# A hybrid attention block: last neighbourhood keys and queries before the last two gates, softmax sums from a ones column in v, gates by row, 368 keys

## The chip, the cores and the metric

The kernel runs on one core of a Trainium2 chip. Six agents matter: TensorE (matmuls, PE in the profile; its weight loads are PEld), VectorE (DVE), ScalarE (ACT), GpSimd (POOL), SyncE (SP), which issues nearly all DMAs here, and the DMA engines. Matmul results land in PSUM, eight banks of 128 partitions by 512 fp32; everything else lives in SBUF. The metric is the device time of one execution in microseconds, as the median of three runs.

## The reference

The kernel computes one encoder layer for 1024 tokens of width 1024, in fp32 accuracy:

```python
h = x @ W_in                       # q_a k_a v_a z_a (512 each), q_b (512) k_b v_b (128 each) z_b (512)
y_a = neighborhood_attention(q_a, k_a, v_a, rel_bias)   # 8 heads of 64, grid of 16 rows x 64 columns, window 8 x 16
y_b = windowed_gqa_with_sink(rotary(q_b), rotary(k_b), v_b, sink)   # 8 query heads, 2 kv heads, |i - j| <= 128
mixed = concat(y_a * silu(z_a), y_b * silu(z_b))
x = layer_norm(2 ** 0.25 * x + mixed @ W_out)
```

In the neighbourhood attention a query at (row, column) sees 8 rows by 16 columns, clamped inside the grid. With tokens put in column-major order (16 rows per column), a block of 128 queries is 8 grid columns, and the keys that any of them can see are 23 columns for an inner block (368 keys), 16 columns for the first and the last block (256 keys).

## The kernel before

**Number format.** Every fp32 operand is split into two fp16 tiles, high part and rest (`hi` and `lo` in the code), and a product takes three matmuls: high x high, high x rest, rest x high. ACT usually makes the high part, DVE or POOL the rest.

**Projections.** `W_in` is cut into 21 slices of 128 output columns, named after what they make: `q0..q3`, `k0..k3`, `z0..z3` for the neighbourhood heads (two heads a slice), `qb0..qb3`, `kb`, `zb0..zb3` for the banded heads. `ORDER` lists them. `project(name)` is a generator of 48 matmuls: two halves of 512 tokens, each 8 k-tiles x 3 matmuls into one of two `pj` PSUM banks. When a half is complete, `evac` queues its evacuation: for k and q `split_k` and `split_q` (L250 on ACT and L256 on DVE, each for two heads, so four operations a half; for k POOL also copies both parts to the other 64 partitions, L298); for z a tanh on ACT (L344) and a product on DVE (L345), the half of a SiLU. A new half waits until the half before the last has left its bank. The first six slices and v are made before the attention starts; the other fifteen fill it.

**Attention.** There are 128 units: 64 of the banded group b, then 64 of the neighbourhood group a, each a head (pair p, head j of it) and a block t of 128 queries. A unit goes through steps on every engine:

- `stage_qk`: two score matmuls (L797, L798) into one of four `s` banks, against 256 or 384 keys; then one DVE operation (L805) adds the bias or mask, takes the row minimum `nm` and writes `sn`.
- `stage_exp`: ACT's exponential (L821) writes back into the bank; its accumulator output (a separate read instruction) gives the row sum into a column of `sm`.
- `stage_tr`, a unit later: ACT and DVE split the probabilities into fp16 high part and rest (L829, L830), and SP issues a transposing DMA (L833).
- `stage_pv`, for four units at once: value matmuls (L856) of the transposed blocks (as weights, with a load each) against v, 64 columns each, 33 for a quad of four units.
- `stage_on`: DVE takes the reciprocal of the four row sums (L862) and multiplies (L865).
- `stage_ot`, after both heads: four PE transposes (L876) and one DVE operation that multiplies the result into the gate tile z (L879 for group b, L882 for group a, where z holds tokens by row and the attention result is by column, so z is addressed with a stride of 64 elements).

v is made first, split into `vt` tiles by ACT and DVE (L695, L686), stored to the DRAM buffer `vd`, and gathered per head pair in column order (`gather_v`, tile `va`). The bias of a head (`bias`, 896 columns for the three kinds of block, `BWIN`) is loaded per head and scaled on POOL (L773).

**What sets the order.** The program order on every engine is written out by hand in the main loop over steps i, one unit a step. `FILL_AT` gives for each filling slice the step at which its 48 matmuls begin, so that slice n is spread over the steps `FILL_AT[n]` to `FILL_AT[n + 1]`; `pump_to` places them between the score matmuls. The four engine queues `queues` hold evacuations and other small work, and a few of these are popped in each step. `m_queue`, `wo_split` and `WO_LD` place the splits of the gated tiles and of `W_out`. From step 121 on the filling work is the first output matmuls (`out_head`, L1002); the rest of them, the residual and the layer norm stand in `final()`, where the last gate, the split of the last gated tile (L910) and eight splits of `W_out` (L961, L967) run on DVE beside output matmuls on PE.

```python
ORDER = ["zb0", "z0", "zb1", "kb", "qb0", "z1", "qb1", "zb2", "qb2", "k0", "qb3", "zb3", "q0", "k1", "q1",
         "k2", "q2", "z2", "k3", "q3", "z3"]
FILL = ORDER[NPRO:]                 # NPRO = 6
FILL_AT = [0, 8, 17, 25, 33, 41, 49, 57, 66, 74, 81, 89, 97, 105, 112, 121, 123.5, 126, 128, 131, 136]
```

Pair p of the neighbourhood group has the units 64 + 16 p to 79 + 16 p.

## Time and profile before

| | |
|---|---|
| median of three runs | 449.97 us (449.89 to 451.79) |
| the profiled execution | 448.97 us |
| its span, first to last instruction | 447.2 us, granted clock 0.997 |
| busy time in the span | PE 437.1, DVE 349.0, ACT 309.9, POOL 212.0 us |
| share of the 16 DMA engines on SP's main queue | 65.8% |
| attention, first to last score matmul | 121.3 to 358.0 us |

Times are counted from the start of the span. Busy time of PE is modelled: a matmul's row lasts from its start to its drained end, and the next one starts earlier, so the distance of starts tells the true rate. A row of a group gives line, engine, operation, tiles and shapes, the number of instructions, then their busy time in us and the mean duration of one in ns, then the engine's idle time just before them and what ended it. A row of waits gives the total, the number of times and the longest. In a timeline the columns are start, duration, engine, line, operation, and in brackets the idle time before with its releaser.

### The profile page before, as it was taken

What the parts mean: (1) busy time and instruction counts of PE and PEld (TensorE: products, weight loads), DVE (VectorE), ACT (ScalarE), POOL (GpSimd) and SP (SyncE); (2) the same over time, 40 slices, a digit from 0 to 9 for tenths busy, and PEclk for the clock granted to TensorE, in tenths of its full rate; (3) what the DMA queues carried; (4) which work ended last, traced back from release to release, by engine and by line L of the source; (5) the groups of instructions that cost most, each with busy time, mean ns of one, the idle gap of its engine ahead of it and who ended that gap; (6) DMA issues with size and microseconds to landing.
All of it is one profiled execution on the core that took longest, in us unless ns stands there. A gap on an engine that the chain in (4) does not pass through costs nothing.

```text
span 447.2 us, 9320 instructions
## 1 busy us (share of the span) xinstructions
PE 437.1 (98%) x3241; PEld 252.9 (57%) x3241; DVE 349.0 (78%) x840; ACT 309.9 (69%) x700; POOL 212.0 (47%) x219
## 2 busy tenths in 40 slices
PE   9999999999999999999999999999979999999995
PEld 8997754444445565555555655555536654444454
DVE  5978867438977898887898888888778847679944
ACT  5759789766599987877867887788777957012401
POOL 0110064637749559766424757565462404304740
PEclk9999999999999999999999999999999999999998
DMA  8921569980169999596986669569669598102711
GB/s 269 391 89 59 170 233 327 319 269 25 53 141 197 212 197 175 105 159 123 166 120 116 130 143 172 93 135 200 131 131 188 102 188 320 47 1 83 247 72 71
DMA packets 123984, 71.21 MB, mean 159 GB/s; under 512 B 96800, under 2 KB 105888, under 8 KB 123936
## 3 DMA queue, kind: packets, MB, share of 16 engines
q1 hardware_dynamic: 123792, 70.48, 65.8%
q8 instruction: 25, 0.41, 0.4%
q14 instruction: 23, 0.19, 0.2%
q10 hardware_dynamic: 144, 0.13, 0.1%
HBM read 41.23 MB, written 6.29 MB: 106 GB/s over the span
## 4 chain that ended last, share of the span: by engine, by line
PE 77%; DVE 10%; ACT 7%; issue 5%; DVEq 0%; ACTq 0%
PE ps_pj L380 36%; PE ps_s L1002 8%; PE ps_s L487 6%; PE ps_pj L1002 5%; PE ps_t L856 5%; PE ps_pj L487 3%; PE ps_t L487 3%; PE ps_t L1002 3%; PE ps_s L797 3%; PE ps_s L798 3%; ACT split L829 3%; ACT ps_s L821 2%; DVE split L830 2%; DVE qs L256 2%; DVE ks L256 1%
## 5 line engine op out<-in xcount | busy, mean ns | idle before, releaser
L380 PE MATMUL ps_pj<-xf,wh 128*128 128x512 f16 x672 | 202.1, 379 | 0.4 <-DVE ks L256 0.4
L380 PE MATMUL ps_pj<-xf,wl 128*128 128x512 f16 x336 | 127.3, 379 | 0.0
L380 PEld LDWEIGHTS <-wh 128*128 128x128 f16 x672 | 63.6, 98 | 61.6 <-DVE ks L256 1.2
L830 DVE SCALAR_TENSOR_TENSOR split<-ps_s,split 128x384 f16<-128x384 f32 (+1 forms) x128 | 66.9, 522 | 28.9 <-ACT split L829 27.5
L821 ACT ACTIVATE ps_s<-sn,nm 128x385 f32<-128x385 f32 (+3 forms) x128 | 71.0, 554 | 26.3 <-DVE nm L805 25.6
L1002 PEld LDWEIGHTS <-m 128*128 128x128 f16 x432 | 40.0, 98 | 41.6 <-DVE m L910 0.7
L829 ACT ACTIVATE split<-ps_s 128x384 f16<-128x384 f32 (+1 forms) x128 | 58.6, 458 | 2.4
L380 PEld LDWEIGHTS <-wl 128*128 128x128 f16 x336 | 32.8, 98 | 37.5
L197 POOL TENSOR_SCALAR wr<-wr,wsc 128x512 f32<-128x512 f32 x26 | 20.5, 789 | 67.7 <-ACT wh L192 61.2
L797 PE MATMUL ps_s<-ks,qs 128*128 128x384 f16 (+1 forms) x128 | 40.0, 313 | 2.9 <-DVE qs L256 2.9
L805 DVE CUSTOM_DVE_ANT_0 sn<-ps_s,bm,nsk 128x384 f32<-128x384 f32 (+1 forms) x64 | 40.7, 636 | 1.4 <-PE ps_s L798 1.2
L1002 PE MATMUL ps_s<-wo,m 128*128 128x512 f16 (+1 forms) x192 | 40.7, 366 | 0.2 <-DVE m L910 0.2
L798 PE MATMUL ps_s<-ks,qs 128*128 128x384 f16 (+1 forms) x128 | 40.0, 313 | 0.0
L805 DVE CUSTOM_DVE_ANT_0 sn<-ps_s,bias,sg 128x384 f32<-128x384 f32 (+1 forms) x64 | 37.0, 578 | 2.6 <-PE ps_s L798 2.0
L856 PEld LDWEIGHTS <-tr 128*128 128x128 f16 x1056 | 35.2, 98 | 2.5
L198 POOL TENSOR_TENSOR wl<-wr,wh 128x512 f16<-128x512 f32 x26 | 32.7, 1256 | 2.2
L298 POOL COPY ks<-ks 64x512 f16<-64x512 f16 x40 | 26.1, 661 | 10.3 <-DVE ks L256 3.4
L197 POOL TENSOR_SCALAR ws<-ws,wsc 128x512 f32<-128x512 f32 x16 | 11.1, 691 | 33.9 <-ACT wh L192 30.1
L1002 PE MATMUL ps_pj<-wo,m 128*128 128x512 f16 (+1 forms) x144 | 26.5, 326 | 0.0
L1101 POOL TENSOR_TENSOR xr<-xr,gb 128x512 f32<-128x512 f32 x7 | 9.8, 1396 | 32.5 <-ACT xr L1098 32.5
L821 ACT ACTIVATION_READ_ACCUMULATOR ps_s<-sn,nm 128x1 f32 x128 | 24.4, 191 | 0.0
L797 PEld LDWEIGHTS <-qs 128*128 128x128 f16 x128 | 12.5, 98 | 18.4 <-DVE qs L256 3.4
(187 smaller groups left out, 800.2 us busy)
## 6 DMA issues: line engine op xcount, KB each, us to landing
ws<-in_wt SPq DMA_DIRECT2D x15, 512.0 KB, 5.8
wr<-in_wt SPq DMA_DIRECT2D x26, 256.0 KB, 3.8
wor<-in_wo SPq DMA_DIRECT2D x22, 256.0 KB, 3.5
xr<-in_x SPq DMA_DIRECT2D x8, 512.0 KB, 9.0
out<-xr SPq DMA_DIRECT2D x15, 256.0 KB, 2.1
bias<-in_bias SPq DMA_DIRECT2D x8, 448.0 KB, 3.9
wvraw<-in_wv SPq DMA_DIRECT2D x9, 320.0 KB, 5.9
xraw<-in_xT SPq DMA_DIRECT2D x11, 256.0 KB, 4.5
```

Source lines behind the costliest of these rows:

```text
L197: nc.gpsimd.tensor_scalar(raw, raw, scale, 1.0, op0=ALU.mult, op1=ALU.mult)
L198: nc.gpsimd.tensor_sub(l, raw, h)
L380: nc.tensor.matmul(ps, a[:, k % 4, :], mv, start=(k == 0 and i == 0), stop=(k == KT - 1 and i == 2))
L487: nc.tensor.matmul(ps[:, :320], lh[:, ts], rh[:, cs], start=(k == ko[0] and i == 0), stop=(k == ko[-1] and i == 2))
L797: nc.tensor.matmul(ps[:, :n], q, sl[0], start=True, stop=False)
L798: nc.tensor.matmul(ps[:, :n], q, sl[1], start=False, stop=True)
L805: nc.vector.tensor_tensor_reduce(sn[:, :n], ps[:, :n], bias_t, sg[:, c:c + 1], init, op0=ALU.add, op1=ALU.min, accum_out=nm)
L821: nc.scalar.activation(pt[:, :m], sn[:, :m], AF.Exp, bias=nm, scale=-1.0, accum_out=sm[:, k:k + 1])
L829: nc.scalar.activation(hl[:, :m, 0, :], src, AF.Copy, scale=PSCALE)
L830: nc.vector.scalar_tensor_tensor(hl[:, :m, 1, :], src, PSCALE, hl[:, :m, 0, :], op0=ALU.mult, op1=ALU.subtract)
L856: nc.tensor.matmul(ps[:, HD * m:HD * m + HD], a, b_, start=(i == 0), stop=(i == len(mms) - 1))
L1002: nc.tensor.matmul(ps, lh[:, ts], rh[:, cs], start=(e == EO[0] and i == 0), stop=(e == EO[-1] and i == 2))
```

## The change

Four edits are made together.

1. *Order.* `k3` and `q3` are projected before `z2`, so that the last three slices are q3, z2, z3; four entries of `FILL_AT` move up by one step, so k2 is spread over 8 steps where it had 7, and z2 over 7.
2. *368 keys.* For inner blocks of group a the score matmuls, the bias addition and the minimum cover 368 keys. The bias tiles lose 16 columns. The last 16 columns of `sn` are filled once with a large value, so that the exponential over 384 columns gives zeros there. The value matmuls of the third key block use 112 partitions, of the transposed weights and of v.
3. *Ones column.* Each head's part of v gets a 65th column that holds 1/2^14 (the inverse of the scale of the split probabilities). In group a the matmuls with the high part of v take 65 columns (the high x high and the rest x high product), those with its rest take 64; column 64 of the result is the row sum. The accumulator output of the exponential is dropped for group a, and the reciprocal reads the sums from PSUM. POOL sets the columns in each of the eight `vt` tiles; the DRAM buffer and the gathers grow from 256 to 260 elements a row.
4. *Gates by row.* The gate of group a runs over z row by row (unstrided), and reads the PSUM result with a stride of 16 elements.

```diff
@@ -25,15 +25,15 @@
 PSCALE = 2.0 ** 14
 MSCALE = 2.0 ** -44
 QSCALE = 2.0 ** -15
-LTT, LPP, BP, BH, BR, ND, NA, NX, F1 = 1, 6, 2, 9, 5, 1, 1, 6, 0.2
+LTT, LPP, BH, ND, NA, NX, F1 = 1, 6, 9, 1, 1, 6, 0.2
 NSPLIT, NP = 6, 2
 ORDER = ["zb0", "z0", "zb1", "kb", "qb0", "z1", "qb1", "zb2", "qb2", "k0", "qb3", "zb3", "q0", "k1", "q1",
-         "k2", "q2", "z2", "k3", "q3", "z3"]
+         "k2", "q2", "k3", "q3", "z2", "z3"]
 NPRO = 6
 NS = 21 - NPRO
 NR = 8
 FILL = ORDER[NPRO:]
-FILL_AT = [0, 8, 17, 25, 33, 41, 49, 57, 66, 74, 81, 89, 97, 105, 112, 121, 123.5, 126, 128, 131, 136]
+FILL_AT = [0, 8, 17, 25, 33, 41, 49, 57, 66, 74, 82, 90, 98, 106, 113, 121, 123.5, 126, 128, 131, 136]
 ZTAG = {"z3": "zv", "zb3": "zc", "z2": "zs", "zb1": "zd", "zb2": "ze"}
 KO = (2, 3, 4, 5, 6, 7, 0, 1)
 X1_AT = ((0,), (1,), (2,), (3, 4), (5,), (6, 7), (), ())
@@ -48,7 +48,8 @@
 WO_AT = [67, 71, 75, 79, 84, 88, 93, 98]
 WO_LD = [16, 22, 19, 25, 36, 39, 42, 45, 48, 112, 116, 28, 130, 130, 130, 130]
 WP = 256
-BWIN = (0, 256, 640, 896)
+BWIN = (0, 256, 624, 880)
+VE = HD + 1
 ROPE_PERM = list(range(0, 16)) + list(range(32, 48)) + list(range(16, 32)) + list(range(48, 64))
 SWAP = list(range(16, 32)) + list(range(0, 16))
 
@@ -69,7 +70,7 @@
         bufs = {"pj": 2, "s": 4, "t": 2}[tag]
         return (ps1 if bufs == 1 else ps2).tile([128, 512], F32, tag=tag, name=f"ps_{tag}", bufs=bufs)
 
-    vd = dram.tile([4, GW, ROWS, 256], F16, name="vd")
+    vd = dram.tile([4, GW, ROWS, 4 * VE], F16, name="vd")
 
     taken = [0]
 
@@ -683,16 +684,17 @@
         def v_part(t):
             if t > 0:
                 vt, v3 = vts.pop(t - 1)
-                nc.vector.scalar_tensor_tensor(vt[:, :, 1, :], v3, vrs, vt[:, :, 0, :], op0=ALU.mult, op1=ALU.subtract)
-                nc.vector.tensor_copy(vb[:, t - 1], vt[:, 8:10])
+                nc.vector.scalar_tensor_tensor(vt[:, :, 1, :HD], v3, vrs, vt[:, :, 0, :HD], op0=ALU.mult, op1=ALU.subtract)
+                nc.vector.tensor_copy(vb[:, t - 1], vt[:, 8:10, :, :HD])
                 for i in range(2):
                     nc.sync.dma_start(
                         vd[:, :, 2 * (t - 1) + i, :].rearrange("q c e -> c q e"),
                         vt[GW * i:GW * i + GW, 0:8].rearrange("p (q h) i e -> p q (h i e)", h=2))
             if t < 8:
-                vt = vp.tile([128, 10, 2, HD], F16, tag=("vt", "wvr")[t % 2], name=f"vt{t}", bufs=3)
+                vt = vp.tile([128, 10, 2, VE], F16, tag=("vt", "wvr")[t % 2], name=f"vt{t}", bufs=3)
                 v3 = v32[t].rearrange("p (h e) -> p h e", e=HD)
-                nc.scalar.activation(vt[:, :, 0, :], v3, AF.Copy, scale=vrs)
+                nc.gpsimd.memset(vt[:, 0:8, :, HD:VE], 1.0 / PSCALE)
+                nc.scalar.activation(vt[:, :, 0, :HD], v3, AF.Copy, scale=vrs)
                 vts[t] = vt, v3
 
         def sum_w(i):
@@ -734,7 +736,7 @@
         return ap.tile(shape, dt, tag="va", name=name, bufs=6)
 
     def gather_v(p):
-        t = va[p] = big_ap([128, 8, 256], F16, f"va{p}")
+        t = va[p] = big_ap([128, 8, 4 * VE], F16, f"va{p}")
         bulk["last"] = bulk["step"]
         nc.sync.dma_start(t, vd[p].rearrange("(k c) r e -> (c r) k e", k=8))
 
@@ -759,8 +761,8 @@
 
     def geom(u):
         g, p, j, t = u
-        lo, hi = max(t - 1, 0), min(t + 2, 8)
-        return 128 * (hi - lo), hi - lo
+        m = min(t + 2, 8) - max(t - 1, 0)
+        return 368 if g == "a" and m == 3 else 128 * m, m
 
     def stage_load(u, i):
         g, p, j, t = u
@@ -797,9 +799,11 @@
         nc.tensor.matmul(ps[:, :n], q, sl[0], start=True, stop=False)
         nc.tensor.matmul(ps[:, :n], q, sl[1], start=False, stop=True)
         s0 = sns[units.index(u) % 2]
-        sn = s0[:, 384 - n:]
+        sn = s0 if g == "a" else s0[:, 384 - n:]
         if g == "b" and t < 2:
             nc.vector.tensor_copy(s0[:, 384:385], nsk[:, h:h + 1])
+        elif g == "a" and p == 0 and j == 0 and t < 2:
+            nc.vector.memset(s0[:, 368:384], -NEG)
         nm = ap.tile([128, 1], F32, tag="nm", name="nm", bufs=6)
         c = min(p, 1) if g == "b" else 2
         nc.vector.tensor_tensor_reduce(sn[:, :n], ps[:, :n], bias_t, sg[:, c:c + 1], init,
@@ -809,23 +813,21 @@
         st[u, "nm"] = nm
 
     def stage_exp(u):
-        n, _c = geom(u)
-        m = n + 1 if u[0] == "b" else n
+        m = 128 * geom(u)[1] + (u[0] == "b")
         sn, nm = st.pop((u, "sn")), st.pop((u, "nm"))
         pt = st.pop((u, "ps"))
         k = units.index(u) % 4
-        if k == 0:
-            st["sm"] = ap.tile([128, 4], F32, tag="sm", name="sm", bufs=4)
-        sm = st["sm"]
-        st[units.index(u) // 4, "sm"] = sm
-        nc.scalar.activation(pt[:, :m], sn[:, :m], AF.Exp, bias=nm, scale=-1.0, accum_out=sm[:, k:k + 1])
+        if k == 0 and u[0] == "b":
+            st[units.index(u) // 4, "sm"] = ap.tile([128, 4], F32, tag="sm", name="sm", bufs=4)
+        acc = st[units.index(u) // 4, "sm"][:, k:k + 1] if u[0] == "b" else None
+        nc.scalar.activation(pt[:, :m], sn[:, :m], AF.Exp, bias=nm, scale=-1.0, accum_out=acc)
         st[u, "p"] = pt
 
     def stage_tr(u):
         n, m = geom(u)
         pt = st.pop((u, "p"))
         hl = split[units.index(u) % NSPLIT]
-        src = pt[:, :n].rearrange("p (k c) -> p k c", c=128)
+        src = pt[:, :128 * m].rearrange("p (k c) -> p k c", c=128)
         nc.scalar.activation(hl[:, :m, 0, :], src, AF.Copy, scale=PSCALE)
         nc.vector.scalar_tensor_tensor(hl[:, :m, 1, :], src, PSCALE, hl[:, :m, 0, :],
                                        op0=ALU.mult, op1=ALU.subtract)
@@ -844,26 +846,30 @@
             g, p, j, t = u
             tr = st.pop((u, "tr"))
             mms = []
-            for i in range(geom(u)[1]):
+            n, c = geom(u)
+            w = VE if g == "a" else HD
+            for i in range(c):
                 k = max(t - 1, 0) + i
+                d = slice(0, min(128, n - 128 * i))
                 if g == "a":
-                    v = [va[p][:, k, 128 * j + 64 * e:128 * j + 64 * e + 64] for e in range(2)]
+                    v = [va[p][d, k, VE * (2 * j + e):VE * (2 * j + e) + (VE, HD)[e]] for e in range(2)]
                 else:
-                    v = [vb[:, k, p // 2, e, :] for e in range(2)]
-                ph, pl = tr[:, 2 * i, :], tr[:, 2 * i + 1, :]
-                mms += [(ph, v[0]), (ph, v[1]), (pl, v[0])]
-            for i, (a, b_) in enumerate(mms):
-                nc.tensor.matmul(ps[:, HD * m:HD * m + HD], a, b_, start=(i == 0), stop=(i == len(mms) - 1))
+                    v = [vb[d, k, p // 2, e, :] for e in range(2)]
+                ph, pl = tr[d, 2 * i, :], tr[d, 2 * i + 1, :]
+                mms += [(ph, v[0], w), (ph, v[1], HD), (pl, v[0], w)]
+            for i, (a, b_, e) in enumerate(mms):
+                nc.tensor.matmul(ps[:, w * m:w * m + e], a, b_, start=(i == 0), stop=(i == len(mms) - 1))
 
     def stage_on(q):
         g, p, j, h = quad(q)
         ps = st.pop((q, "o"))
         ri = ap.tile([128, 4], F32, tag="ri", name="ri", bufs=4)
-        nc.vector.reciprocal(ri, st.pop((q, "sm")))
+        w = VE if g == "a" else HD
+        o = ps[:, :4 * w].rearrange("p (m e) -> p m e", e=w)
+        nc.vector.reciprocal(ri, o[:, :, HD] if g == "a" else st.pop((q, "sm")))
         if j == 0:
             on[g, p, h] = ap.tile([128, 4, 2, HD], F32, tag="on", name="on", bufs=2)
-        nc.vector.tensor_mul(on[g, p, h][:, :, j, :], ps[:, :4 * HD].rearrange("p (m e) -> p m e", e=HD),
-                             ri.unsqueeze(2).to_broadcast([128, 4, HD]))
+        nc.vector.tensor_mul(on[g, p, h][:, :, j, :], o[:, :, :HD], ri.unsqueeze(2).to_broadcast([128, 4, HD]))
 
     def stage_ot(q):
         g, p, j, h = quad(q)
@@ -878,8 +884,8 @@
             z = zt[4 + p][:, 512 * h:512 * h + 512]
             nc.vector.scalar_tensor_tensor(z, ps, z_col(4 + p), z, op0=ALU.mult, op1=ALU.mult)
         else:
-            z = zt[p].rearrange("p (r c) -> p c r", c=GW)[:, 32 * h:32 * h + 32, :]
-            nc.vector.scalar_tensor_tensor(z, ps.rearrange("p (c r) -> p c r", r=ROWS), z_col(p), z,
+            z = zt[p].rearrange("p (r c) -> p r c", c=GW)[:, :, 32 * h:32 * h + 32]
+            nc.vector.scalar_tensor_tensor(z, ps.rearrange("p (c r) -> p r c", r=ROWS), z_col(p), z,
                                            op0=ALU.mult, op1=ALU.mult)
 
     run_to(48 * NPRO)
```

## The prediction

> **What bounds the kernel now.** I read the head of the page first, then the busy time of each engine in five stretches of the second half, where all the edits act. Columns of the second view: stretch, its length, then busy time and number of instructions of PE, PEld, DVE, ACT, POOL, granted clock, DMA share, GB/s.
>
> ```profile
> span 447.2 us, 9320 instructions
> PE 437.1 (98%) x3241; PEld 252.9 (57%) x3241; DVE 349.0 (78%) x840; ACT 309.9 (69%) x700; POOL 212.0 (47%) x219
> ```
>
> ```profile
> 272.00:311.00 39.00, 39.00 (x343) 22.19 (x342) 33.80 (x88) 32.72 (x83) 23.07 (x26) 1.00 0.84 151
> 311.00:334.00 23.00, 20.06 (x160) 10.88 (x159) 18.26 (x46) 16.77 (x44) 13.90 (x18) 1.00 0.61 124
> 372.00:386.00 14.00, 13.78 (x65) 6.14 (x64) 13.74 (x18) 7.99 (x10) 9.36 (x6) 1.00 0.47 186
> ```
>
> TensorE at full clock sets the time, and time can go in two ways: fewer columns streamed, or its few holes closed. Busy rows hide small holes, because each matmul's row is longer than the distance to the next start. So I look at starts. The timeline (start, duration, engine, line, operation, idle before and what ended it) shows the three holes of the second half:
>
> ```profile
> 269.76 0.38 PE L380 MATMUL ps_pj<-xf,wl 128*128 128x512 f16 x1
> 269.97 0.33 PE L797 MATMUL ps_s<-ks,qs 128*128 128x384 f16 x1
> ...
> 270.30 1.13 PE L856 MATMUL ps_t<-va,tr 128*128 128x64 f16 x33
> 271.81 0.61 PE L380 MATMUL ps_pj<-xf,wh 128*128 128x512 f16 x2 [0.39 <-DVE ks L256]
> ...
> 293.84 1.12 PE L856 MATMUL ps_t<-va,tr 128*128 128x64 f16 x33
> 294.81 0.59 PE L380 MATMUL ps_pj<-xf,wh 128*128 128x512 f16 x2
> ...
> 330.53 0.38 PE L380 MATMUL ps_pj<-xf,wl 128*128 128x512 f16 x1
> 330.74 0.69 DVE L256 SCALAR_TENSOR_TENSOR qs<-ps_pj,qs 64x512 f16<-64x512 f32 x1
> 333.11 0.68 DVE L256 SCALAR_TENSOR_TENSOR qs<-ps_pj,qs 64x512 f16<-64x512 f32 x1 [0.68 <-ACT qs L250]
> 333.85 0.28 PE L797 MATMUL ps_s<-ks,qs 128*128 128x256 f16 x1 [2.94 <-DVE qs L256]
> ...
> 384.14 0.38 PE L1002 MATMUL ps_t<-wo,m 128*128 128x512 f16 x1
> 384.74 0.39 PE L1002 MATMUL ps_s<-wo,m 128*128 128x512 f16 x1 [0.22 <-DVE m L910]
> ```
>
> A 512-column matmul is followed after 0.21 us (269.76 to 269.97; 0.216 over longer runs), a block of 33 value matmuls after 0.97 (293.84 to 294.81), that is 29 ns each. By these pitches the holes are: **3.10 us** (333.85 less 330.53 less 0.216), where unit 112, the first of the last neighbourhood pair, waits for the last DVE half of q3; **0.54 us** (271.81 less 270.30 less 0.97), where a projection waits for a PSUM bank that DVE is still emptying of k2; **0.38 us** (384.74 less 384.14 less 0.216) at the end, where the output matmuls wait for DVE's split of the last gated mixer tile.
>
> **The change part by part.** Groups, shapes kept apart: count, busy us, mean ns of one, idle before and its releaser.
>
> ```profile
> L797 PE MATMUL ps_s<-ks,qs 128*128 128x384 f16 x96 | 31.3, 326 | 0.0
> L797 PE MATMUL ps_s<-ks,qs 128*128 128x256 f16 x32 | 8.7, 273 | 2.9 <-DVE qs L256 2.9
> L856 PEld LDWEIGHTS <-tr 128*128 128x128 f16 x1056 | 35.2, 98 | 2.5
> L805 DVE CUSTOM_DVE_ANT_0 sn<-ps_s,bias,sg 128x384 f32<-128x384 f32 x48 | 29.3, 611 | 1.8 <-PE ps_s L798 1.4
> L805 DVE CUSTOM_DVE_ANT_0 sn<-ps_s,bias,sg 128x256 f32<-128x256 f32 x16 | 7.7, 479 | 0.8 <-PE ps_s L798 0.6
> L821 ACT ACTIVATION_READ_ACCUMULATOR ps_s<-sn,nm 128x1 f32 x128 | 24.4, 191 | 0.0
> L862 DVE RECIPROCAL ri<-sm 128x4 f32<-128x4 f32 x32 | 5.4, 168 | 0.0
> L882 DVE SCALAR_TENSOR_TENSOR z<-ps_t,zc,z 128x512 f32<-128x512 f32 x8 | 9.3, 1168 | 7.4 <-PE ps_t L876 7.4
> L879 DVE SCALAR_TENSOR_TENSOR z<-ps_t,zc,z 128x512 f32<-128x512 f32 x8 | 6.0, 747 | 0.0
> L345 DVE SCALAR_TENSOR_TENSOR z<-z,ps_pj 128x512 f32<-128x512 f32 x10 | 6.9, 689 | 2.5 <-ACT z L344 2.3
> L256 DVE SCALAR_TENSOR_TENSOR ks<-ps_pj,ks 64x512 f16<-64x512 f32 x16 | 11.0, 686 | 0.3
> L250 ACT ACTIVATE ks<-ps_pj 64x512 f16<-64x512 f32 x16 | 9.4, 585 | 5.0 <-DVE ks L256 5.0
> L344 ACT ACTIVATE z<-ps_pj,invt 128x512 f32<-128x512 f32 x10 | 6.8, 682 | 5.6 <-PE ps_pj L380 3.8 <-POOL rp_raw L316 1.8
> ```
>
> *Order (k3, q3 ahead of z2).* No PE work is added or dropped; 192 matmuls change places. q3 fills units 98 to 106 instead of 105 to 112, so its last split ends about 6 units, some 10 us, before unit 112 asks for it. What is late next for unit 112? In the trace the bias scaling and the copy of k3 to the other partitions:
>
> ```profile
> 325.38 1.01 POOL L773 TENSOR_SCALAR bias<-bias,rsg 128x896 f32<-128x896 f32 x1
> ...
> 328.36 0.61 POOL L298 COPY ks<-ks 64x512 f16<-64x512 f16 x1
> ```
>
> Both end (326.39, 328.97) before 330.75, when PE is free, and k3's copies move ahead as well. So all 3.10 us go. k2 gets units 74 to 82, where it had 74 to 81: each half of it has half a unit more (0.8 us at the 1.62 us between unit starts there), which covers the 0.54 us hole. z2 now ends at unit 113; its consumer, the gate of pair 2, comes at units 117 and 121, so 4 units cover ACT's 0.68 and DVE's 0.69 twice. It takes the short seven-unit window, and costs its bank one ACT and one DVE operation per half where q3 cost two of each.
>
> What it costs: between units 90 and 98 k3 replaces z2 on the engines. DVE gets 4 x 0.686 for 2 x 0.689, that is +1.37 us, ACT 4 x 0.585 for 2 x 0.682, +0.98. Queued behind them are the score reductions and splits that free the four score banks, and there the slack is small:
>
> ```profile
> 297.95 0.56 DVE L830 SCALAR_TENSOR_TENSOR split<-ps_s,split 128x384 f16<-128x384 f32 x1 [0.26 <-ACT split L829]
> 298.53 0.69 DVE L345 SCALAR_TENSOR_TENSOR z<-z,ps_pj 128x512 f32<-128x512 f32 x1
> 299.24 0.27 PE L797 MATMUL ps_s<-ks,qs 128*128 128x256 f16 x1
> ```
>
> Unit 92's bank is free at 298.51, and unit 96 takes it at 299.24: 0.73 us. Against +1.37 on DVE stand the savings below (0.19 us of ACT in every unit, which DVE's splits wait for, and 0.42 of DVE at each of two gates of units 82 to 90). I put the new holes at 0.5, with bounds 0 and 1.4 (the 1.37 with no saving).
>
> *368 keys.* 96 score matmuls (48 units, two each) lose 16 columns. (326 - 273)/128 = 0.41 ns a column, so 96 x 16 x 0.41 = **-0.64 us** on the path. DVE's reduction loses 16 x 1.03 ns in 48 units, 0.8 us off the path. The two fills of 16 columns on DVE are shorter than a reciprocal (168 ns), and cost nothing beside the rows above.
>
> *Ones column.* 352 value matmuls stream 65 columns: 352 x 0.41 ns = **+0.15 us**. ACT loses 64 accumulator reads, 64 x 191 ns = 12.2 us; PE did not wait for ACT, so this buys slack and no time. The reciprocal reads PSUM and now waits for the value matmuls; the multiply after it on DVE waited for them before, so nothing is queued longer. POOL gets eight small memsets in front of its weight splits at 66 to 80 us, and two of ACT's value casts wait for them; POOL and ACT both idle there, and PE waits for neither:
>
> ```profile
> 79.94 0.69 ACT L341 ACTIVATE z<-ps_pj,inv 128x512 f32<-128x512 f32 x1 [0.87 <-PE ps_pj L380]
> 81.50 0.73 POOL L197 TENSOR_SCALAR wr<-wr,wsc 128x512 f32<-128x512 f32 x1 [4.86 <-ACT wh L192]
> ```
>
> Without that cover it would be at most 8 x 0.17 (the reciprocal's row), 1.3 us. SP's stores and gathers of v grow by 4 columns in 256; the first gather comes 50 units after the last store.
>
> Two things no row shows. The third block of each such unit loads weights on 112 partitions, and the second-half values start at odd fp16 addresses. The price of either lies between 0 and the rival's below; I take 0, since the rows of neither matmul nor load depend on anything but columns here.
>
> *Gates by row.* The gate strides z by 64 elements now (1168 ns); the one of the other group, unstrided, takes 747. Afterwards z is contiguous and PSUM is read with a stride. The k split reads PSUM with a stride too and takes 686, where the unstrided z product takes 689, so I take 747: 0.42 us less, eight times. Only the last one is on the path: DVE runs without a break from it to the split that PE waits for at 384.74, so the 0.38 us hole closes (**-0.38**; bounds 0 and 0.38).
> [...]
>
> *Sum.* -3.10 - 0.54 - 0.38 - 0.64 + 0.15 + 0.50 = **-4.0 us**. The profiled execution took 448.97 (span 447.2 and 1.8 around it); the three runs shown have a median of 449.97, 1.0 above it. I apply the difference to the median: **446.0**. With no new hole it is 445.5, with 1.4 of them and the end hole left 447.3.
>
> **The rivals.**
> *Slower: weight loads on 112 partitions lose their overlap.* The place is the third block of 48 units, 48 x 3 = 144 loads. A load's row is 98 ns, but pairs follow each other at 29 ns, so loads overlap. If a short one did not, it would cost 98 - 29 = 69 ns, 144 x 69 = 9.9 us: 455.9. It decides from 28 ns a load on (4.0/144). For it: no load here has fewer than 128 partitions. Against: nothing in these rows depends on partitions.
> [...]
> *No change: odd addresses halve the read of values.* 176 matmuls (the second half of v) would take 64 x 0.41 = 26 ns more, 4.6 us: 450.6. All moving operands of the trace start at even addresses, so it can't be excluded.
> *The change does not do what it says: the hole moves.* If DVE falls so far behind in units 90 to 106 that PE waits there for k3's and q3's splits, 4 x 0.69 = 2.8 us come back: 448.8. For it: the slack of 0.73. Against: DVE idles in the same stretch (33.80 of 39.00 busy).
>
> **How the numbers follow.** No change is about 0.5%, 2.25 us: 447.7 to 452.2. Forecast 0.77, all of it but a sliver faster; moved hole 0.09 and odd addresses 0.05, both within 0.5%; short loads 0.07, slower; 0.02 for anything else slower. That gives faster 0.77, same 0.14, slower 0.09. The range runs from 444.7 (all holes closed, no new one, 445.5, less the 0.8 by which a median of three can sit nearer to the profiled time) to the moved hole, 448.8; outside are the odd addresses and the short loads, 0.14.
>
> **What would show it.** Right: no idle of PE before L797's counterpart at unit 112, nor before the output matmul after the last split; score matmuls some 6.6 ns shorter; gates near 0.75; 64 fewer accumulator reads on ACT. Wrong: blocks of 33 value matmuls that take clearly over 0.98 us (short loads or odd addresses), or new PE idle behind ks or qs between units 90 and 106.

## The result and the profile after

The changed kernel takes **447.86 us** (median of 7 runs, 447.65 to 449.00) against 450.86 (7 runs, 449.89 to 452.65) for the kernel before beside it on the same chip: ratio 0.9938, 95% interval 0.9917 to 0.9959, that is 3.0 us less where 4.0 were forecast. (The 449.97 from which the forecast started is the median of the first three of these seven.) The profiled execution took 447.86 (the one before 448.97), so the two traces differ by 1.1 us only; where the rest of the 3.0 us lies is told below, at the clock. The page of the changed kernel begins:

```profile
span 446.1 us, 9265 instructions
...
PE 438.3 (98%) x3241; PEld 254.7 (57%) x3241; DVE 346.8 (78%) x842; ACT 302.6 (68%) x636; POOL 211.7 (47%) x227
```

The span fell and TensorE's busy time rose: idle was closed, and matmuls became dearer. (Lines after the edits shift by one to six: L797 is L799 now, L856 is L861.) The timeline of TensorE at the places of the three old holes, unit 112 at 331.44 and the end at 384.34:

```profile
331.01 0.59 PE L381 MATMUL ps_pj<-xf,wh 128*128 128x512 f16 x2
331.44 0.27 PE L799 MATMUL ps_s<-ks,qs 128*128 128x256 f16 x1
331.55 0.27 PE L800 MATMUL ps_s<-ks,qs 128*128 128x256 f16 x1
...
383.91 0.59 PE L1008 MATMUL ps_t<-wo,m 128*128 128x512 f16 x2
384.34 2.75 PE L1008 MATMUL ps_s<-wo,m 128*128 128x512 f16 x12
```

Two matmuls of 512 columns last 0.43 us from start to start, and 331.01 + 0.43 is 331.44: nothing is lost at unit 112, nor at the end (383.91 + 0.43), nor at k2. The idle now stands mainly at three other places (timeline of all engines, cut to these rows):

```profile
99.21 0.63 ACT L213 ACTIVATE junk<-wr 128x512 bf16<-128x512 f32 x1
...
99.29 0.38 PE L381 MATMUL ps_pj<-xf,wl 128*128 128x512 f16 x1
...
99.98 0.16 PE L219 MATMUL ps_t<-wm,ones 128*128 128x2 bf16 x1 [0.31 <-ACT junk L213]
...
302.75 0.38 PE L381 MATMUL ps_pj<-xf,wl 128*128 128x512 f16 x1
303.21 0.32 PE L799 MATMUL ps_s<-ks,qs 128*128 128x368 f16 x1
303.37 0.32 PE L800 MATMUL ps_s<-ks,qs 128*128 128x368 f16 x1
303.94 0.60 PE L381 MATMUL ps_pj<-xf,wh 128*128 128x512 f16 x2 [0.26 <-DVE ks L257]
...
326.48 0.38 PE L381 MATMUL ps_pj<-xf,wl 128*128 128x512 f16 x1
327.23 0.61 PE L381 MATMUL ps_pj<-xf,wh 128*128 128x512 f16 x2 [0.37 <-DVE qs L257]
```

At 99 us the matmul of `w_scale` waits for the sums of the weights on ScalarE; at 303 a score bank and then a `pj` bank are late because of k3; at 326 z2's second half waits for the bank of q3's second half. By distances of starts, less the pitch of each form (the same working as in the prediction), the two traces and a second profile of the changed kernel (label after_again) lose, in us:

| place | before | changed | changed, again |
|---|---|---|---|
| unit 112, k2, end | 3.10, 0.55, 0.38 | 0 | 0 |
| 99 us, before L219 | 0 | 0.48 | 2.48 |
| 242 us (k1) | 0.17 | 0.60 | 0.19 |
| 303 us (k3) | 0 | 0.67 | 0.66 |
| 326 us (z2's second half) | 0 | 0.54 | 0.53 |
| value matmuls of group a, over 29 ns each | 0.1 | 1.2 | 1.2 |

The groups of the edited lines (count, busy us, mean ns, idle before and releaser):

```profile
L799 PE MATMUL ps_s<-ks,qs 128*128 128x368 f16 x48 | 15.3, 319 | 0.1
...
L823 ACT ACTIVATION_READ_ACCUMULATOR ps_s<-sn,nm 128x1 f32 x64 | 12.2, 190 | 0.0
...
L861 PEld LDWEIGHTS <-tr 112*128 112x128 f16 x144 | 7.7, 97 | 0.0
...
L888 DVE SCALAR_TENSOR_TENSOR z<-ps_t,zc,z 128x512 f32<-128x512 f32 x8 | 6.0, 748 | 7.4 <-PE ps_t L882 7.4
...
L696 POOL MEMSET vt<- 128x16 f16 x8 | 1.0, 192 | 2.2 <-DMA vd<-vt 2.2
```

### The profile page after: what moved, and what is told of

Same layout as the page of the kernel before. It is cut to its first block, busy times and chain, and to the rows that moved or that the text cites. A ratio compares the mean times of both kernels' runs of the same rounds, so it can differ in the third digit from the quotient of the medians.

```text
span 446.1 us, 9265 instructions
## 1 busy us (share of the span) xinstructions
PE 438.3 (98%) x3241; PEld 254.7 (57%) x3241; DVE 346.8 (78%) x842; ACT 302.6 (68%) x636; POOL 211.7 (47%) x227
## 4 chain that ended last, share of the span: by engine, by line
PE 82%; ACT 5%; DVE 4%; DMA 4%; issue 3%; POOL 1%; SPq 0%; DVEq 0%; POOLq 0%; ACTq 0%
PE ps_pj L381 36%; PE ps_s L1008 9%; PE ps_s L488 6%; PE ps_t L861 6%; PE ps_pj L1008 5%; PE ps_t L1008 5%; PE ps_s L799 3%; PE ps_s L800 3%; PE ps_pj L488 3%; PE ps_t L488 3%; DMA vd<-vt 2%; DMA ws<-in_wt 2%; ACT split L831 1%; PE ps_t L882 1%; DVE qs L257 1%
## 5 line engine op out<-in xcount | busy, mean ns | idle before, releaser
L799 PE MATMUL ps_s<-ks,qs 128*128 128x384 f16 (+2 forms) x128 | 39.7, 310 | 0.1
L800 PE MATMUL ps_s<-ks,qs 128*128 128x384 f16 (+2 forms) x128 | 39.7, 310 | 0.0
L809 DVE CUSTOM_DVE_ANT_0 sn<-ps_s,bias,sg 128x368 f32<-128x368 f32 (+1 forms) x64 | 36.2, 565 | 3.8 <-PE ps_s L800 3.2
L861 PEld LDWEIGHTS <-tr 128*128 128x128 f16 (+1 forms) x1056 | 36.2, 98 | 2.4
L1107 POOL TENSOR_TENSOR xr<-xr,gb 128x512 f32<-128x512 f32 x7 | 9.8, 1398 | 32.5 <-ACT xr L1104 32.5
L1008 PE MATMUL ps_t<-wo,m 128*128 128x512 f16 x96 | 22.8, 379 | 0.0
L488 PEld LDWEIGHTS <-xf 128*128 128x128 f16 x192 | 18.6, 98 | 7.2
```

Source lines behind the costliest of these rows:

```text
L488: nc.tensor.matmul(ps[:, :320], lh[:, ts], rh[:, cs], start=(k == ko[0] and i == 0), stop=(k == ko[-1] and i == 2))
L799: nc.tensor.matmul(ps[:, :n], q, sl[0], start=True, stop=False)
L800: nc.tensor.matmul(ps[:, :n], q, sl[1], start=False, stop=True)
L809: nc.vector.tensor_tensor_reduce(sn[:, :n], ps[:, :n], bias_t, sg[:, c:c + 1], init, op0=ALU.add, op1=ALU.min, accum_out=nm)
L861: nc.tensor.matmul(ps[:, w * m:w * m + e], a, b_, start=(i == 0), stop=(i == len(mms) - 1))
L1008: nc.tensor.matmul(ps, lh[:, ts], rh[:, cs], start=(e == EO[0] and i == 0), stop=(e == EO[-1] and i == 2))
```

## The experiments

### The parts of the change

First the changed kernel again, for the spread of its holes:

> The changed kernel once more, to stand beside the parts of the change on the same chip. By the start-to-start ledger of its profile TensorE has 1.1 us more holes than forecast behind the splits of k3 and q3 and at units 64 to 66, 0.5 us more at 99 us, and about 1 us in longer value matmuls. If these belong to the kernel, the same holes stand in this profile (0.25 + 0.42 us near 303 us, 0.54 us near 326 us); if they are chance, they lie elsewhere or are gone. Time about 3 us below the kernel before.

Measured: 448.87 us (12 runs) against 450.94 (29 runs), ratio 0.9959 (0.9941 to 0.9976). The holes at 303 and 326 us are those of the first profile; the one at 99 us is five times as long. The gain is 2.1 to 3.0 us.

Then the order alone, on the kernel before (`ORDER` and `FILL_AT` as in the diff of the change, nothing else; five entries of `FILL_AT` move up there, not four):

> The kernel before with the new order and the new start steps alone. Ledger theory: the hole of 3.10 us at unit 112 and the 0.54 us hole of k2 go, the 0.38 us hole at the end stays, and 1 to 1.5 us of new holes come where k3 and q3 empty their banks: 2.0 to 2.7 us faster than before. Rival (the order pays only with ACT relieved of the accumulator reads): ACT's 191 ns per unit push DVE further back in units 90 to 106, the new holes grow to 2.5 us and more, and the gain is under 1 us.

Measured: 449.19 us, ratio 0.9978 (0.9961 to 0.9996). No idle at unit 112 nor at 99 us, but z2's second half waits 1.11 us for q3's bank, k3 costs about 0.75 us at 305, k2 still 0.23, about ten holes of 0.1 to 0.4 us stand between 217 and 303 us, and the end hole stays. The profiled execution took 450.74 us, the longest of the twelve, so not every one of these holes need stand in the others. By the medians the order alone is worth 1.75 us, and not the 3.1 us (3.10 + 0.54 less 0.50) that I gave it.

The other three edits without the order (`ORDER` and `FILL_AT` put back):

> The changed kernel with the old order and the old start steps: 368 keys, ones column and gates by row alone. Ledger theory: the hole at unit 112 is back (3 us, ended by the last q split); 368 keys give 0.6, the gate 0.4, the value matmuls take back 0.9 to 1.1: within 0.5 us of the kernel before. Rival (the three edits pay by relieving ACT and DVE): the q splits come earlier by the relief, the hole at unit 112 shrinks below 2.5 us, and the time is 1 us or more under before.

Measured: 450.43 us, ratio 1.000 (0.998 to 1.002). They bring nothing together, though 368 keys shorten the matmuls by 0.62 us and unit 112 waits less (timeline of TensorE):

```profile
333.67 0.38 PE L381 MATMUL ps_pj<-xf,wl 128*128 128x512 f16 x1
335.51 0.28 PE L799 MATMUL ps_s<-ks,qs 128*128 128x256 f16 x1 [1.46 <-DVE qs L257]
```

That is 1.62 us (1.84 less the pitch) for 3.10. The likely reason is the relief of ScalarE and VectorE, which I had called slack without time: it took 1.5 us off this hole. No run tells the accumulator reads from the gates and the 368 keys in it. 1.92 us at 99 us, 1.1 us in the value matmuls and 1.2 us in small holes between 227 and 245 us ate what was gained.

The gate by column again, in the changed kernel:

```diff
-            z = zt[p].rearrange("p (r c) -> p r c", c=GW)[:, :, 32 * h:32 * h + 32]
-            nc.vector.scalar_tensor_tensor(z, ps.rearrange("p (c r) -> p r c", r=ROWS), z_col(p), z,
+            z = zt[p].rearrange("p (r c) -> p c r", c=GW)[:, 32 * h:32 * h + 32, :]
+            nc.vector.scalar_tensor_tensor(z, ps.rearrange("p (c r) -> p c r", r=ROWS), z_col(p), z,
```

> The changed kernel with the gates of the neighbourhood group by column again (z with a stride of 64 elements). Forecast's mechanism: the gate takes 1168 ns instead of 748, and the hole of about 0.38 us before the output matmul after the last split (near 384 us) is back. Rival: the hole at the end was closed by something else, and stays closed.

Measured: one execution of 450.21 us. The gate takes 1175 ns, and the end hole is back, as a wait of 0.25 us in the row and 0.42 us between starts; the hole at 99 us was 1.92 us here too.

```profile
386.03 0.39 PE L1008 MATMUL ps_s<-wo,m 128*128 128x512 f16 x1 [0.25 <-DVE m L916]
```

### The hole at 99 us

It stands in every kernel so far with the column of ones in the rows of v, and in none without. SP's queue between 60 and 100 us, by what it waited for (total us, times, longest; two rows of each list), before:

```profile
SPq L181 <- POOL wl L198: 14.8, 8, 2.9
SPq L689 <- DVE vb L687: 2.1, 3, 1.1
```

and in the changed kernel, with the last three loads `ws` of its timeline:

```profile
SPq L640 <- DMA vd<-vt: 1.8, 1, 1.8
SPq L690 <- DMA vd<-vt: 1.4, 2, 0.9
```
```profile
90.11 3.13 SPq L640 DMA_DIRECT2D ws<-in_wt  x3
```

Before, SP waited for no store of v there. In the built program each DMA issue also waits for one of eight counters in turn (in the traces before and after, SP's 281 issues come back to the same semaphore every eight, and none starts before the one eight ahead of it has landed), that is for the landing of the issue eight before; 16 stores of v share SP's queue with the loads of `ws` and `wr`. Two causes were left: the memsets on GpSimd, or stores that land late. The ones written by ScalarE:

```diff
-                nc.gpsimd.memset(vt[:, 0:8, :, HD:VE], 1.0 / PSCALE)
                 nc.scalar.activation(vt[:, :, 0, :HD], v3, AF.Copy, scale=vrs)
+                nc.scalar.activation(vt[:, 0:8, :, HD:VE].rearrange("p h i e -> p h (i e)"), v3[:, 0:8, 0:2],
+                                     AF.Copy, scale=0.0, bias=1.0 / PSCALE)
```

> The changed kernel, with the column of ones written into vt by ScalarE (an activation of 128x16 behind each vt) and no longer by a memset on GpSimd. What is asked is the hole of 0.5 to 2.5 us that TensorE shows at 99 us in every kernel with the column of ones, before the matmul of w_scale (L219). Theory A, GpSimd's queue: the memsets of the last vt tiles wait there for the stores of the tiles before (2.2 us), the wl parts and with them the wr loads stand behind. Then the hole goes, TensorE loses nothing at 99 us and the kernel is 0.5 to 2.5 us faster than the changed one. Theory B, SP's queue: the stores of 520-byte rows land later (6.1 to 6.5 us against 4.9), SP's next issues wait for landings and the last ws loads come late. Then the move does nothing: a hole of 0.5 to 2.5 us stays at 99 us, SP still waits for vd<-vt, and the time is that of the changed kernel within 0.5 us.

The rows of 512 bytes kept, the ones set in `va` after the order lo, hi, hi, lo (the core of the edit):

```diff
+                for j in range(2):
+                    nc.vector.scalar_tensor_tensor(vt[:, :, 3 * j, :], v3[:, :, j, :], vrs, vt[:, :, 1 + j, :],
+                                                   op0=ALU.mult, op1=ALU.subtract)
-        t = va[p] = big_ap([128, 8, 4 * VE], F16, f"va{p}")
-        nc.sync.dma_start(t, vd[p].rearrange("(k c) r e -> (c r) k e", k=8))
+        t = va[p] = big_ap([128, 8, 258], F16, f"va{p}")
+        nc.gpsimd.memset(t[:, :, 128:129], 1.0 / PSCALE)
+        src = vd[p].rearrange("(k c) r e -> (c r) k e", k=8)
+        nc.sync.dma_start(t[:, :, 0:128], src[:, :, 0:128])
+        nc.sync.dma_start(t[:, :, 129:257], src[:, :, 128:256])
...
+                    v = [va[p][d, k, 64 + 64 * j:129 + 64 * j], va[p][d, k, 193 * j:193 * j + 64]]
```

> The changed kernel, with vt and vd kept at 512-byte rows as before the change: the pieces of a row lie lo, hi, hi, lo, and the gather takes two pieces of 256 bytes into a 258-wide row of va, between which one column is set to one (four small memsets on GpSimd instead of eight). Theory B (520-byte stores land late and hold SP): landing of vd<-vt falls back to about 4.9 us, SP waits for no vd<-vt, ScalarE waits for the last ws loads less than 1 us as in the kernel before, the hole at 99 us is gone. Theory A would say the same of the hole here, and is told apart by the run with the ones on ScalarE. Both: span 444.5 to 446, ratio to the kernel before 0.989 to 0.993. If the hole stays, neither is right. The value matmuls of 65 columns now start even in both heads, the 64-column ones of the second head odd: their excess over 29 ns should halve at least if the odd start is what costs.

And the pieces 66 apart, 65 used (`VE = HD + 2`), so that each starts at an even element:

> The changed kernel with the pieces of v stored 66 wide instead of 65 (66 columns apart, still 65 or 64 used), so that every piece starts at an even fp16 element. If the odd starts cost the 3.8 ns per 64-column and 2.2 ns per 65-column matmul seen over 29 ns, the excess of the 128x64 matmuls (0.48 us) goes to about 0 and that of the 65-column ones falls by half or more; the 112-row ones keep what the short weight load costs. If it stays, the start is not the cause. The rows are 528 bytes, so theory B has the hole at 99 us stay; theory A too.

The landing of the stores of v (least, median, longest), in the order before, changed, ones_act, dense, even66:

```profile
DMA to landing us min/median/max: 3.1/4.9/7.1
```
```profile
DMA to landing us min/median/max: 4.8/6.5/8.4
```
```profile
DMA to landing us min/median/max: 4.6/7.5/8.7
```
```profile
DMA to landing us min/median/max: 3.5/4.5/8.0
```
```profile
DMA to landing us min/median/max: 3.9/6.0/7.2
```

Measured: ones_act 449.81 us (ratio 0.9982, 0.9961 to 1.0003) with 1.65 us of idle at 99 us and SP still waiting for `vd<-vt`: the memsets are not the cause. **dense 446.88 us, ratio 0.9918 (0.9894 to 0.9941)**: SP waits for no store, no idle at 99 us, 4.1 us less than before. What SP waited for on a DMA there is one row:

```profile
SPq L692 <- DMA ws<-in_wt: 0.5, 2, 0.3
```

In even66 (one execution, 446.94 us) 528-byte rows landed in 6.0 us and the hole was absent, against my expectation: SP waited 0.9 us for stores. The hole goes with the landing over all traces with wider rows: medians of 6.0, 6.5, 7.0, 7.3, 7.4, 7.4, 7.5 and 7.8 us stand beside holes of 0, 0.48, 0.33, 1.68, 1.92, 1.92, 1.65 and 2.48 us. So the cause is how late the stores land and hold SP's queue, and some 1 us of landing decides whether the sums are late.

What it is about the wider rows that makes them land later (medians of 6.5 and 7.5 us against 4.9) is not shown: rows of 520 bytes laid end to end are longer than those of 512 and also start at other addresses, and no run here tells the start from the length, nor 520 from 528 bytes.

The room for the column alone, in the kernel before (65-wide pieces in `vt`, `vd`, `va`, the column set and never used):

> The kernel before, with nothing of the change but the room for it: pieces of v 65 wide instead of 64 in vt, vd and va (rows of 520 bytes, the column set by GpSimd's memset and never used); order, sums, gates and 384 keys as before, value matmuls of 64 columns. Theory B (520-byte stores land late, and SP, which waits for the landing of the issue eight before, brings the last ws loads late): landing of vd<-vt 6 to 8 us, a hole of 0.5 to 2.5 us at 99 us, and 0.5 to 2.5 us slower than the kernel before, if the hole at unit 112 stays at 3.1 us. Its rival, that the hole comes of something else in the change: no hole at 99 us, same time as before. On the value matmuls: if the layout costs (odd starts, pieces that lie across), the middle one of three takes 33 ns here too; if the mixture of 65 and 64 columns costs, all take 29 ns.

Measured: 453.24 us against 451.08, ratio 1.0052 (1.0025 to 1.0078): 2.2 us slower. The stores landed in 7.0 us, the hole at 99 us was 0.33 us. The value matmuls of group a, 64 columns as before, cost 0.9 us more (the busy row). Some 0.4 us of this are 15 matmuls at the end of the stretch with a granted clock of 0.56 that is told below; without them it is 0.6 us over 29 ns each, and the pitch of the middle one of three is 32.5 ns for 29:

```profile
L858 PE MATMUL ps_t<-va,tr 128*128 128x64 f16 x528 | 18.9, 194 | 0.0
...
L858 PE MATMUL ps_t<-vb,tr 128*128 128x64 f16 x528 | 18.0, 193 | 0.0
```

So the layout of v alone, with no 65th column in any matmul, costs 0.6 of the 1.1 us. The rest stands in the first one of three, which takes 31.3 ns in the changed kernel (33.1 in the blocks of 112 partitions) and 29.2 here; no run separates the 65 columns, the 112 partitions and the change of width from one matmul to the next. It isn't the odd start: in even66 the middle matmul takes 32 to 33 ns with an even one. In dense it is the middle one of the second head and the last one of the first that take 32 to 33 ns, and the sum is 1.0 us. What about the layout does it is open.

The profile of this kernel has one thing more. Stretches of the span (length, busy time and count of PE, PEld, DVE, ACT, POOL, granted clock, DMA share, GB/s), then TensorE's timeline from the hole on:

```profile
331.00:335.00 4.00, 1.26 (x6) 0.39 (x4) 3.21 (x8) 2.20 (x8) 1.48 (x2) 1.00 0.56 100
335.00:338.00 3.00, 2.98 (x10) 1.28 (x11) 1.52 (x4) 2.47 (x6) 0.64 (x1) 0.56 1.14 297
```
```profile
331.88 0.38 PE L381 MATMUL ps_pj<-xf,wl 128*128 128x512 f16 x1
335.02 0.28 PE L799 MATMUL ps_s<-ks,qs 128*128 128x256 f16 x1 [2.76 <-DVE qs L257]
...
335.25 0.97 PE L381 MATMUL ps_pj<-xf,wh 128*128 128x512 f16 x2
336.01 0.63 PE L381 MATMUL ps_pj<-xf,wl 128*128 128x512 f16 x1
336.44 1.06 PE L381 MATMUL ps_pj<-xf,wh 128*128 128x512 f16 x2
```

After the hole of 2.93 us at unit 112 the granted clock was 0.56 for 3 us and the pitch of 512 columns up to 0.43 us: 1.7 us lost on top of the hole. In the profile of the kernel before the hole of 3.10 us had no such sequel; the stretch behind it there, with a granted clock of 1.00 and a pitch of 0.216 us:

```profile
334.00:337.00 3.00, 3.00 (x45) 2.00 (x44) 2.15 (x6) 2.46 (x7) 0.81 (x1) 1.00 1.12 294
```

What decides whether a lower clock follows such a hole is not shown: it did after 2.93 us of idle in one execution and did not after 3.10 in another.

The mean granted clock of each execution shows how often the kernel before loses clock. Of the 74 executions of it that ran beside the experiments, 27 have a clock of 0.997 or 0.998 and take 448.8 to 450.8 us, with a median of 449.4; the other 47 have 0.995 or less and take 450.6 to 453.9, with a median of 451.3. The loss in the profile of pad_only should lower the mean by some 0.004, an estimate from its 1.7 us in 450, and that profile's own mean is 0.994. 8 of the 10 executions of pad_only, which has the hole too, have 0.994 or less. Of the 77 executions of the changed kernel and the other repeated kernels, whose hole at unit 112 is gone or at most 1.7 us, 10 have 0.995 or less.

So the kernel before loses another 1.9 us in most of its executions, and its profiled one (0.997) is of the kind that doesn't. That is why the runs gain more than the traces. That the loss stands at unit 112 in the kernel before too is argued from pad_only; no trace of the kernel before shows it. Beside the executions of the kernel before with 0.997 or more on the same chip, the median of after_again is 0.5 us shorter, order_only 0.2 us, dense 2.9, before_hi2 (below) 2.3 and best_hi2 (below) 3.9, and order_back is 1.1 us longer. By this reading, closing or halving the hole at unit 112 paid twice, by its length and by the clock.

### The holes that came with the order

z2 given eight units and z3 seven (`106, 113, 121` to `106, 114, 121` in `FILL_AT`), in the changed kernel:

> The changed kernel with z2 given eight units (106 to 114) instead of seven, z3 seven instead of eight. z2's second half then starts half a unit later, about 2 us, and must wait for the bank of q3's second half no more: the hole of 0.54 us at 326 us goes, if it is the early start that makes it. What stays is 0.1 us or less. The holes at 99 and 242 and 303 us stay as they are. Span 0.3 to 0.6 us shorter than the changed kernel with the same hole at 99 us; if z3 in seven units opens another hole of its own, no gain.

Measured: one execution, 449.57 us, with 0.22 us at 329 us for 0.54 (0.1 or less was expected) and 1.68 us at 99 us. The short window of z2 was somewhat over half of the cause. The same with dense (label best):

> The kernel with 512-byte rows of v and the ones set in va (dense), with z2 given eight units and z3 seven. The two mendings lie at different places (99 us and 326 us) and should add: no hole at 99 us, 0.2 us or less at 326 us, the holes at 242 and 302 us (0.2 and 0.7 us) as they were. Span 444.3 to 444.9, ratio to the kernel before 0.988 to 0.993, at or under that of dense alone. If z3 in seven units or a shifted place opens holes of its own, the same as dense.

Measured: 447.01 us, ratio 0.9922 (0.9891 to 0.9953): no better than dense (0.9918). In its profile, which is of the longest of the six executions (448.00 us), 0.68 us remained at 303 us and 0.59 us at 242 us, most of it for banks that ScalarE and VectorE were emptying of k, and three holes of 0.2 to 0.3 us. The prediction's row of L250 held the reason: 5.0 us in which ScalarE waited for VectorE, that is 8 second high parts of 16 that came only after VectorE's rest of the first head. One token lets ScalarE take both:

```diff
-        pop("act", 1, 0)
+        pop("act", 2, 0)
         pump_to(i + F1)
```

> The same, and ScalarE takes the high parts of both heads of a k or q half in one go, ahead of the unit's other work, where it took one, waited for VectorE's rest of that head and took the other. If the evacuation of a bank is long because of this to and fro (8 of 16 second high parts waited for VectorE), the holes before the next projection group (0.42 us at 302 us, what is left at 242 and 326 us) close: 0.3 to 0.8 us less than best. If ScalarE's two 0.58 us operations in a row hold up the exponentials instead, the score units wait, holes of 0.2 to 0.5 us come at each of the 16 halves and it is 0.5 to 2 us slower.

Measured: **445.37 us (6 runs, 444.98 to 445.89) against 451.08, ratio 0.9883 (0.9849 to 0.9916)**, 1.64 us less than best where 0.3 to 0.8 were expected. Two lines of its page (span, and the chain that ended last by engine), and all waits of TensorE in this kernel:

```profile
span 443.6 us, 9275 instructions
...
PE 99%; DVE 0%; ACT 0%; issue 0%; ACTq 0%
```
```profile
PE ps_t L1093 <- ACT dr L1091: 1.8, 1, 1.8
PE ps_t L414 <- DVE warm L121: 1.0, 1, 1.0
```

Every hole of 0.1 us or more between the first and the last microseconds is closed. The last run asks whether the order was needed at all: the same token in the kernel before.

> The kernel before, with nothing of the change: only ScalarE takes the high parts of both heads of a k or q half in one go. Theory of the prediction (the 3.10 us at unit 112 come of the order: q3's second half is evacuated after the neighbourhood keys are due): the place of q3 is the same, so most of the hole stays, 2 us or more, and the time is the kernel before's within 1 us (ratio 0.998 to 1.001). Rival (the to and fro of ScalarE and VectorE over a bank makes each evacuation late, and the order only moved the place where that shows): the hole falls to 1.5 us or less, those of 0.55 us at 271 us and 0.2 us at 241 us close, ratio 0.990 to 0.996, as much as the whole change brought, without it. If ScalarE's two operations in a row hold up the exponentials, new holes and no gain.

Measured: **447.17 us against 450.53, ratio 0.9925 (0.990 to 0.995)**, 3.4 us less: as much as the whole change, from one token (2.0 us by the two traces; the rest goes with the clock, 0.996 or more in all six executions). Its unit 112 (timeline of TensorE and ScalarE):

```profile
329.95 0.38 PE L380 MATMUL ps_pj<-xf,wl 128*128 128x512 f16 x1
331.89 0.28 PE L797 MATMUL ps_s<-ks,qs 128*128 128x256 f16 x1 [1.56 <-DVE qs L256]
```
```profile
324.64 1.18 ACT L250 ACTIVATE qs<-ps_pj 64x512 f16<-64x512 f32 x2
...
330.54 0.57 ACT L250 ACTIVATE qs<-ps_pj 64x512 f16<-64x512 f32 x1
331.01 0.36 ACT L829 ACTIVATE split<-ps_s 128x256 f16<-128x256 f32 x1
331.86 0.59 ACT L250 ACTIVATE qs<-ps_pj 64x512 f16<-64x512 f32 x1 [0.48 <-DVE qs L256]
```

The hole is 1.72 us for 3.10 and those at 241 and 271 us are gone; the one at the end stays (0.36). The result lies between the two theories: about 1.4 us of the hole were late evacuations, 1.7 are the order's. q3's first half leaves in one go (two operations from 324.64); at unit 112 `need` pulls the second half out in the old to and fro.

## Why the prediction was right or wrong

The forecast of 446.0 us was 1.9 too low, inside its range (444.7 to 448.8): 0.9 of this is its starting point (449.97 for 450.86), 1.0 the gain (3.0 for 4.0). That the gain came so near is in part luck. By the traces, of which its sum is made, the change is worth 1.1 us and not 4.0; the other 1.9 us goes with the clock that the kernel before loses in most of its executions, which no term of the sum names. Its terms, as the profiles show them:

- *Hole at unit 112, -3.10*: right, no idle at 331.44. But the cause was told by half: before_hi2 and order_back take 1.4 to 1.5 us off it with q3 in its old place.
- *k2, -0.54, and end, -0.38*: right. The end hole returns with the gate by column (0.42). The gate came to 748 ns where 747 was taken, with PSUM read at a stride of 16 elements.
- *368 keys, -0.64*: right. The pitch of a score matmul is 156 ns for 162.5, and 96 times 6.5 ns is 0.62 us.
- *Weight loads on 112 partitions, 0*: right within 0.2 us. 144 of them have a row of 97 ns for 98. The value matmuls of the third block follow each other at 31.6 ns on average and those of 128 rows at 31.0; the first of three takes 33.1 ns for 30.6. The rival had 69 ns a load.
- *65 columns, +0.15*: mis-sized, the value matmuls as a whole cost +1.1. The step that failed is "the rows of neither matmul nor load depend on anything but columns here": all v of that trace lay in pieces of 128 bytes, so those rows couldn't show another layout. The rival of odd addresses had the right place for the larger part, and a wrong size (4 ns, not 26) and a wrong name.
- *New holes, +0.50 with bounds 0 and 1.4*: mis-sized, +1.6 in the first profile (0.67 at 303, 0.54 at 326, 0.43 more at 242) and +1.2 in the second. The 303 us were expected behind k3; the 326 us came from a sentence that looked at the wrong half: z2's second half waits for the bank of **q3's** second half, and z2's own cheaper evacuation doesn't help it.
- *Stores and memsets of v, 0*: wrong, and in the second profile the largest error (0.5 and 2.5 us). "The first gather comes 50 units after the last store" names who needs the data, not who is queued behind the store. SP's later issues were, and the weight sums behind them. With 512-byte rows the same change gave 4.1 us by the medians (2.2 by the traces).
- *Accumulator reads, slack and no time*: not shown. They may be part of the 1.5 us that order_back took off unit 112. With the order, order_only has 1.11 us before z2's second half and ten small holes where the changed kernel has 0.54 us and few; but its traced execution was its longest, and no run takes the reads away alone.

Added up: -3.10 - 0.55 - 0.38 - 0.64 + 1.1 + 1.6 + 0.48 is -1.5, and the profiled executions differ by 1.1 (0.3 more stand in the first 45 us). The runs gained 2 to 3 us; what lies between goes with the lower mean clock of the kernel before (0.995 or less in 47 of its 74 executions). The rival "the hole moves" came true in part: 1.2 us behind k3 and q3, not 2.8.

## What to carry to other kernels

When the rows of a DMA get wider (here 520 bytes for 512, and 6.5 us to landing for 4.9), ask what is queued behind it on its queue and whose landing later issues wait for, not only when its data is needed. A row that says which engine an evacuation waited for (here ScalarE for VectorE, 5.0 us in 8 waits) is a lead even when that engine isn't the bound: here one token in the order of two engines was worth the whole change. When the runs gain more than the traces, compare the granted clock of the single executions: a hole that a change closes may have cost more than its length (in the trace of pad_only 1.7 us on top of 2.93). Rows whose instructions all share one layout say nothing about another layout.

## What was not expected of the hardware

- Stores of 520-byte rows landed in 6.5 to 7.8 us where those of 512 bytes took 4.5 to 5.0 (medians), in all kernels here.
- A value matmul of 64 columns took 32 to 33 instead of 29 ns in one place of three once the pieces of v were 65 or 66 wide, at even starts too.
- A hole of 2.93 us was followed by 3 us at a granted clock of 0.56 in one execution, and in 47 of 74 executions of the kernel before, with a hole of 3.10 us in its profile, the mean clock was 0.995 or less and the time 1.9 us longer.
- VectorE's gate with a stride of 16 elements on the PSUM side took 748 ns, the unstrided one 746.
